# q times k-transposed for 96 heads on one core: which pieces of a block and of a head move at the same time

## The chip, the cores and the metric

The kernel runs on one NeuronCore of a Trainium2 chip. Its time is the device time in microseconds, and the median of three runs is what counts. A core has TensorE (PE) for matmuls, VectorE (DVE), ScalarE (ACT) and GpSimd (POOL) for elementwise work, SyncE (SP), which here only issues DMAs, and sixteen DMA engines that carry all traffic between DRAM and the on-chip memory SBUF.

## The reference

For 8 x 12 = 96 heads, q and k are 1024 x 64 in float32, and each head's output is the 1024 x 1024 matrix of all dot products, in float32:

```python
return np.einsum('bhid,bhjd->bhij', q, k).astype(np.float32)
```

So 50.3 MB are read and 402.7 MB are written.

## The kernel before

**Blocks.** The heads are worked through in blocks of 2, 2, 4, 8 and then five times 16 heads (`sizes`; the blocks have the numbers 0 to 8). Each engine's instructions are written out in the order in which it runs them; an engine waits for another by counting semaphores (`Engine.run`, `Engine.wait`).

**Loads.** A block's q (x = 0) and k (x = 1) are loaded by one DMA each into `x_sb` (`Block.load`, L161). The rows of a block are taken as 128 equal pieces, one for each SBUF partition; in a block of 16 heads a piece is 128 rows of 64 floats, 32 KB, so one head is eight pieces and partition p holds piece p. The first blocks are loaded by SP into a free output buffer or into `x_sb`. The loads of the blocks of 16 are issued from ScalarE's queue, q at head 1 and k at head 7 of the block before (L411; `LOADS` for the early ones), and each waits until the casts have read what it overwrites.

**Cast and transpose.** The matmul needs the 64 values of a row along partitions, so q and k are turned. GpSimd casts to float16, four instructions of 32 partitions to each chunk, into one of three `half` buffers (`cast_quads`, L210). VectorE then transposes every 32 x 32 square of a chunk in one instruction (`transpose_quads`, L229) and writes with a stride into `qT` or `kT`. A block of 16 takes four of these for q and four for k, done while the block before is computed (`TURNS`, L408), and the first head of a block waits for all of them. The first two blocks are transposed by TensorE instead (L243).

A partition's quad (32 partitions) decides where its rows go: heads 0 to 7 of a block land on rows 0 to 63 of `qT` and `kT`, heads 8 to 15 on rows 64 to 127.

**Scores.** For each head (`scores`), TensorE loads 128 rows of q as weights (L308) and multiplies them with k in two pieces of 512 (L311); with eight weight loads this gives the 1024 x 1024 result. The weights are every eighth row of the head, so that output partition m gets rows 8m to 8m+7. The PSUM halves take two of the eight parts each, and ScalarE copies each 128 x 2048 half to the output buffer (L288), four copies to a head. There are three output buffers `o_sb` of 4 MB.

**Stores.** When a head is copied, SP issues one DMA of 4096 KB (L301). Output partition p holds the contiguous 32 KB of rows 8p to 8p+7, so again partition p is piece p of the head:

```python
dma = nc.sync.dma_start(
    out=of[self.first + n].rearrange("(p t) j -> p (t j)", p=P),
    in_=buf.rearrange("p t j -> p (t j)"),
)
```

ScalarE's first copy into a buffer waits until the store that last used it has landed.

Of the kernel before, what the change touches and what calls it, by code (L numbers as in the profile page):

```python
# [8 lines left out]
P = 128  # L9
# [50 lines left out]
def kernel(  # L60
# [6 lines left out]
    nc = tc.nc  # L67

    B, H, S, D = q.shape
    NT = S // P  # L70
# [4 lines left out]
    of = out.rearrange("b h i j -> (b h) i j")  # L75
# [3 lines left out]
    NMAX = max(sizes)  # L79
# [26 lines left out]
    class Ring:  # L106


        def __init__(self, bufs):
            self.bufs, self.n = bufs, 0  # L110
            self.busy = [[] for _ in bufs]
# [11 lines left out]
    n, at = S * D // P * 2, 8 * S // 2  # L123
# [13 lines left out]
    class Block:  # L137
        def __init__(self, i, first, N):
            self.i, self.first, self.N = i, first, N
            self.by_pe = i < PE_BLOCKS  # L140
            self.R = N * S // P
            self.elems = self.R * D
            self.cut = max(1, -(-self.R * 32 // CHUNK))
            self.raw = [None] * 2
            self.landed = [[] for _ in range(2)]
            self.rows = [None] * 2
            self.halves = {}
            self.qk = qk_sb[i % 2]
            self.ready = []
            self.over = []  # L150

        def load(self, x, eng, landing=None):
            events = []
            if self.raw[x] is None:
                at = x * self.elems if self.i == EARLY else 0
                self.raw[x] = x_sb[:, at : at + self.elems]
                landing = input_landing[x]
                events = list(input_busy)
            src = flat[x][self.first * S : (self.first + self.N) * S]
            eng.wait(events)  # L160
            dma = eng.eng.dma_start(  # L161
                out=self.raw[x], in_=src.rearrange("(p r) d -> p (r d)", p=P)
            )
            self.landed[x].append(landing.start(dma))

        def load_head(self, n, x, eng, landing):
# [54 lines left out]
        def transpose_quads(self, x, part, c):  # L221
            buf, cast, busy = self.halves.pop((x, part, c))
            n, m = self.N * S // 4, self.R // self.cut
            dst = self.qk[x][:, part * n : (part + 1) * n].rearrange(
                "c (i r) -> c r i", i=32
            )[:, c * m : (c + 1) * m]
            before = blocks[self.i - 2].over if self.i >= 2 else []
            done = dve.run(
                lambda: nc.vector.transpose(  # L229
                    out=dst, in_=buf.rearrange("p (r i) -> p r i", i=32)  # L230
                ),
                [cast] + before,
            )
            busy.append(done)
            self.ready.append(done)
# [17 lines left out]
            self.ready.append(done)  # L253

        def scores(self, n, side, regions, w):
            half, g = divmod(n, self.N // 2)
            cs = slice(half * D, (half + 1) * D)
            qT = self.qk[0].rearrange("c (g m t) -> c g t m", t=NT, m=P)
            kT = self.qk[1].rearrange("c (g j) -> c g j", j=S)
            buf, out_free, out_busy = outs.next()  # L260
            written = {}
            for u in range(NT // w):
                ps, ps_free, ps_busy = regions.next()
                first = True
                for tt in range(w):
                    stationary = qT[cs, g, w * u + tt]
                    done = pe.run(
                        lambda: load_weights(stationary, half * D),
                        self.ready if n == 0 and u == 0 else [],
                        signal=False,  # L270
                    )
                    for j in range(2):
                        at = tt * S + j * 512
                        done = pe.run(
                            lambda: multiply(
                                ps[:, at : at + 512],
                                stationary,
                                kT[cs, g, j * 512 : (j + 1) * 512],
                                half * D,
                            ),  # L280
                            ps_free,
                            signal=tt == w - 1 and j == 1,
                        )
                dst = buf[:, w * u : w * u + w].rearrange("p t j -> p (t j)")
                by_dve = w == 1 and u % 2
                copier = dve if by_dve else act
                copied = copier.run(
                    lambda: (nc.vector.tensor_copy if by_dve else nc.scalar.copy)(  # L288
                        out=dst, in_=ps[:, : w * S]
                    ),  # L290
                    out_free + [done],
                )
                written[copier] = copied
                ps_busy.append(copied)
                for do in side.get(u, []):
                    do()
            self.over = [done]
            sp.wait(written.values())
            if self.first + n == 0:
                sp.wait(blocks[EARLY].landed[0])  # L300
            dma = nc.sync.dma_start(  # L301
                out=of[self.first + n].rearrange("(p t) j -> p (t j)", p=P),
                in_=buf.rearrange("p t j -> p (t j)"),
            )
            out_busy.append(store_landing[id(buf)].start(dma))

    def load_weights(stationary, at):
        return nc.tensor.ldweights(stationary, tile_position=(at, 0))  # L308

    def multiply(dst, stationary, moving, at):  # L310
        return nc.tensor.add_instruction(  # L311
            mybir.InstMatmult(
                name=nc.get_next_instruction_name(),
                ins=[nc.tensor.lower_ap(moving), nc.tensor.lower_ap(stationary)],
                outs=[nc.tensor.lower_ap(dst)],
                start_tensor_calc=True,
                stop_tensor_calc=True,
                ldweights=False,
                tile_position=(at, 0),
                tile_size=(D, P),  # L320
            )
        )
# [33 lines left out]
    for x in range(2):  # L356
# [7 lines left out]
                out=ident,  # L364
                in_=ident,
# [100 lines left out]
```

## Time and profile before

| | |
|---|---|
| median of 3 runs | 1062.69 us (1061.64 to 1063.31) |
| the profiled execution: its time, its span | 1062.84 us, 1061.0 us |
| DMA | 453.21 MB, mean 427 GB/s |
| ScalarE copies (L288), 128 x 2048 | 380, mean 1868 ns |
| VectorE transposes (L229), 128 x 2048 | 22 to qT, mean 9478 ns; 22 to kT, mean 9539 ns |
| GpSimd casts (L210), 32 x 2048 | 176, mean 1888 ns |
| store of a head, 4096 KB, issue to landing | 96, median 21.8 us |
| load of a block of 16, 4096 KB | 5 of q and 5 of k, median 24.1 and 24.3 us |

The page divides the span into 40 slices: each digit of an engine's row is its busy share of a slice in tenths, and the row of GB/s is what the DMA engines moved. The chain of waits follows the work back from the last instruction to what released each step. In a row of the waits stand the engine and line that waited, what it waited for, the microseconds in all, how often, and the longest. A row of the table by stretches has the stretch, its length, each engine's busy time and instructions, the granted TensorE clock, the DMA share and the GB/s. A queue's name with q (ACTq, SPq) is an engine's own sequencer, which issues the DMAs.

### The profile page before, as it was taken

To read this page: it belongs to the slowest core of one execution; us is meant where nothing else is said; L and a number is where in the kernel's file an instruction comes from. 1 tells how busy PE (TensorE), PEld (TensorE's weight loads), DVE (VectorE), ACT (ScalarE), POOL (GpSimd) and SP (SyncE) were. 2 spreads that over 40 slices of the span, in tenths; PEclk is the share of its full clock that TensorE was granted. 3 is DMA by queue.
4 is the path that set the end of the run, shared out by engine and by line. 5 is a ranking of instruction groups with operands and counts; after the bars stand their busy time and mean duration, and the time that the engine had idled before them with its cause. 6 is when DMAs were issued, how large, how long until landed. Compare 5 with 4: busy or idle time off the path is not lost.

```text
span 1061.0 us, 3307 instructions
## 1 busy us (share of the span) xinstructions
PE 700.2 (66%) x1568; PEld 127.3 (12%) x800; DVE 431.0 (41%) x55; ACT 697.1 (66%) x386; POOL 354.2 (33%) x206
## 2 busy tenths in 40 slices
PE   6876744957477748567765856775584777778770
PEld 1111100111011101011111101111110111111110
DVE  2995939029193009339003907600761920000000
ACT  4766655857477747567756756775675777777771
POOL 7927465056380028064006509100913700000000
DMA  9999999999999999999999999999999999999997
GB/s 376 434 435 435 434 434 434 416 421 432 431 434 434 435 429 428 426 435 432 432 422 434 435 427 433 433 434 423 433 429 432 435 434 431 434 434 431 432 431 322
DMA packets 17009, 453.21 MB, mean 427 GB/s; under 512 B 1888, under 2 KB 1888, under 8 KB 2912
## 3 DMA queue, kind: packets, MB, share of 16 engines
q1 hardware_dynamic: 14976, 410.00, 89.7%
q10 hardware_dynamic: 2016, 42.99, 9.8%
q8 instruction: 9, 0.15, 0.0%
q14 instruction: 8, 0.07, 0.0%
HBM read 50.33 MB, written 402.65 MB: 427 GB/s over the span
## 4 chain that ended last, share of the span: by engine, by line
DMA 65%; ACT 16%; PE 7%; DVE 5%; POOL 4%; issue 1%; ACTq 0%; SPq 0%
DMA out_dram<-o_sb 60%; ACT o_sb L288 16%; PE ps_all L311 7%; DVE kT L229 4%; POOL half L210 3%; DMA x_sb<-in_k_dram 2%; DMA x_sb<-in_q_dram 2%; DVE qT L229 1%; DMA o_sb<-in_q_dram 0%; PE ps_all L243 0%; POOL qT L181 0%; DVE kT L250 0%; ACT kT L250 0%; ACTq L36 0%; SPq L169 0%
## 5 line engine op out<-in xcount | busy, mean ns | idle before, releaser
L288 ACT COPY o_sb<-ps_all 128x2048 f32<-128x2048 f32 (+1 forms) x384 | 694.8, 1859 | 333.5 <-DMA out_dram<-o_sb 290.2
L311 PE MATMUL ps_all<-kT,qT 64*128 64x512 f16 x1536 | 696.1, 617 | 328.6 <-ACT o_sb L288 312.8
L210 POOL CAST half<-x_sb 32x2048 f16<-32x2048 f32 x176 | 332.3, 1888 | 482.1 <-DMA x_sb<-in_q_dram 302.2
L229 DVE STREAM_TRANSPOSE qT<-half 128x2048 f16<-128x2048 f16 x22 | 202.6, 9478 | 268.1 <-POOL half L210 268.1
L229 DVE STREAM_TRANSPOSE kT<-half 128x2048 f16<-128x2048 f16 x22 | 202.5, 9539 | 137.5 <-POOL half L210 137.5
L308 PEld LDWEIGHTS <-qT 64*128 64x128 f16 x768 | 124.2, 162 | 897.4 <-issue 878.0
L229 DVE STREAM_TRANSPOSE kT<-kT 128x1024 f16<-128x1024 f16 x2 | 9.4, 4870 | 0.0
L229 DVE STREAM_TRANSPOSE qT<-qT 128x1024 f16<-128x1024 f16 x2 | 9.2, 4780 | 0.0
L210 POOL CAST qT<-o_sb 32x1024 f16<-32x1024 f32 x8 | 8.3, 1035 | 1.2 <-DMA o_sb<-in_q_dram 0.8
L210 POOL CAST kT<-o_sb 32x1024 f16<-32x1024 f32 x8 | 8.3, 1035 | 0.5
L250 DVE COPY qT<-ps_all 128x1024 f16<-128x1024 f16 x2 | 2.4, 1224 | 11.1 <-PE ps_all L243 11.1
L288 DVE COPY o_sb<-ps_all 128x1024 f32<-128x1024 f32 x4 | 4.9, 1225 | 4.4 <-PE ps_all L311 4.4
L243 PE MATMUL ps_all<-ident,qT 128*128 128x128 f16 x16 | 2.1, 311 | 6.8 <-POOL qT L181 6.7
L250 ACT COPY kT<-ps_all 128x1024 f16<-128x1024 f16 x1 | 1.0, 1012 | 4.8 <-PE ps_all L243 4.8
L181 POOL CAST qT<-o_sb 128x512 f16<-128x512 f32 x4 | 2.3, 615 | 3.7 <-DMA o_sb<-in_q_dram 3.7
L250 ACT ACT_TABLE_LOAD x1 | 1.3, 1283 | 2.8 <-issue 2.8
L250 DVE COPY kT<-ps_all 128x1024 f16<-128x1024 f16 x1 | 1.2, 1225 | 4.4 <-PE ps_all L243 4.4
L243 PE MATMUL ps_all<-ident,kT 128*128 128x128 f16 x16 | 2.0, 305 | 0.7 <-ACT o_sb L288 0.7
L181 POOL CAST kT<-o_sb 128x512 f16<-128x512 f32 x4 | 2.4, 618 | 0.3 <-DMA o_sb<-in_q_dram 0.3
L243 PEld LDWEIGHTS ps_all<-ident,qT 128*128 128x128 f16 x16 | 1.5, 141 | 7.1 <-POOL qT L181 7.1
L243 PEld LDWEIGHTS ps_all<-ident,kT 128*128 128x128 f16 x16 | 1.5, 136 | 3.3 <-POOL qT L210 1.6
L359 POOL MEMSET ident<- 128x128 f16 x1 | 0.2, 205 | 0.5 <-SPq L98 0.5
(5 smaller groups left out, 0.7 us busy)
## 6 DMA issues: line engine op xcount, KB each, us to landing
out_dram<-o_sb SPq DMA_DIRECT2D x96, 4096.0 KB, 21.8
x_sb<-in_q_dram ACTq DMA_DIRECT2D x5, 4096.0 KB, 24.1
x_sb<-in_k_dram ACTq DMA_DIRECT2D x5, 4096.0 KB, 24.3
x_sb<-in_q_dram SPq DMA_DIRECT2D x1, 2048.0 KB, 14.6
x_sb<-in_k_dram SPq DMA_DIRECT2D x1, 2048.0 KB, 19.5
o_sb<-in_k_dram ACTq DMA_DIRECT2D x4, 256.0 KB, 4.8
o_sb<-in_q_dram SPq DMA_DIRECT2D x4, 256.0 KB, 5.1
o_sb<-in_q_dram SPq DMA_DIRECT2D x1, 1024.0 KB, 8.2
```

Of the source, the lines that this page charges most:

```text
L181: lambda: nc.gpsimd.tensor_copy(out=rows[:, :, h], in_=self.raw[x][:, h * n : (h + 1) * n].rearrange("p (r d) -> p r d", d=D),),
L210: lambda: nc.gpsimd.tensor_copy(out=dst[q0 : q0 + 32].rearrange("p (r d) -> p r d", d=32), in_=raw[32 * b : 32 * b + 32, c * m : (c + 1) * ...
L229: lambda: nc.vector.transpose(out=dst, in_=buf.rearrange("p (r i) -> p r i", i=32)),
L243: lambda: nc.tensor.transpose(t_ps[:, t], rows[:, t], ident),
L250: lambda: copy(out=dst, in_=t_ps.rearrange("c t m -> c m t")), [done]
L288: lambda: (nc.vector.tensor_copy if by_dve else nc.scalar.copy)(out=dst, in_=ps[:, : w * S]),
L308: return nc.tensor.ldweights(stationary, tile_position=(at, 0))
L311: return nc.tensor.add_instruction(mybir.InstMatmult(name=nc.get_next_instruction_name(), ins=[nc.tensor.lower_ap(moving), nc.tensor.lower ...
L359: cleared = gps.run(lambda: nc.gpsimd.memset(ident, 0.0))
```

## The change

For blocks of 16 heads (`spread`), the piece that goes with a partition is another one. Partition p = 8e + b, with e from 0 to 15 and b from 0 to 7, now holds piece 16b + e of the block (loads) or of the head (stores), where it held piece 8e + b. If a DMA engine e carries the partitions 8e to 8e+7 in order, the sixteen engines now move sixteen neighbouring pieces at a time, and before moved pieces that lie eight apart. The DRAM side of these DMAs has the shape 16 x 8 x 32 KB instead of 128 x 32 KB; the SBUF side stays 128 x 32 KB. The smaller blocks keep the old order for both loads and stores.

All else follows from it. In a load the partitions of e hold parts of all even heads (e below 8) or of all odd heads, so heads now alternate between rows 0 to 63 and rows 64 to 127 of `qT` and `kT` (`scores`). The transposes write to other places, so that k's columns stand in order and the weights (every eighth column of `qT`) give output partition 8e + b the rows of piece 16b + e. No instruction is added or removed, and every engine has its instructions in the order that it had.

```diff
+            self.spread = N == NMAX
...
-            dma = eng.eng.dma_start(
-                out=self.raw[x], in_=src.rearrange("(p r) d -> p (r d)", p=P)
-            )
+            if self.spread:
+                src = src.rearrange("(b e r) d -> e b (r d)", b=NT, e=P // NT)
+            else:
+                src = src.rearrange("(p r) d -> p (r d)", p=P)
+            dma = eng.eng.dma_start(out=self.raw[x], in_=src)
...
-            dst = self.qk[x][:, part * n : (part + 1) * n].rearrange(
-                "c (i r) -> c r i", i=32
-            )[:, c * m : (c + 1) * m]
+            if self.spread:
+                src = buf.rearrange("p (r e b) -> p r e b", e=4, b=NT)
+                if x == 0:
+                    dst = self.qk[x].rearrange("c (b f q e t) -> c q f t e b", b=NT, q=2, e=4, t=NT)
+                    dst = dst[:, part, c * m // NT : (c + 1) * m // NT]
+                    src = src.rearrange("p (f t) e b -> p f t e b", t=NT)
+                else:
+                    dst = self.qk[x].rearrange("c (b q e r) -> c q r e b", b=NT, q=2, e=4)
+                    dst = dst[:, part, c * m : (c + 1) * m]
+            else:
+                dst = self.qk[x][:, part * n : (part + 1) * n]
+                dst = dst.rearrange("c (i r) -> c r i", i=32)[:, c * m : (c + 1) * m]
+                src = buf.rearrange("p (r i) -> p r i", i=32)
...
-                lambda: nc.vector.transpose(
-                    out=dst, in_=buf.rearrange("p (r i) -> p r i", i=32)
-                ),
+                lambda: nc.vector.transpose(out=dst, in_=src),
...
-            half, g = divmod(n, self.N // 2)
+            if self.spread:
+                g, half = divmod(n, 2)
+            else:
+                half, g = divmod(n, self.N // 2)
...
-            dma = nc.sync.dma_start(
-                out=of[self.first + n].rearrange("(p t) j -> p (t j)", p=P),
-                in_=buf.rearrange("p t j -> p (t j)"),
-            )
+            dst, src = of[self.first + n], buf.rearrange("p t j -> p (t j)")
+            if self.spread:
+                dst = dst.rearrange("(b e t) j -> e b (t j)", b=P // 16, t=NT)
+            else:
+                dst = dst.rearrange("(p t) j -> p (t j)", p=P)
+            dma = nc.sync.dma_start(out=dst, in_=src)
```

## The prediction

> **What bounds the kernel now.** I read the page first: busy shares, the forty slices, then the chain.
>
> ```profile
> span 1061.0 us, 3307 instructions
> ...
> DVE 2995939029193009339003907600761920000000
> ...
> DMA  9999999999999999999999999999999999999997
> GB/s 376 434 435 435 434 434 434 416 421 432 431 434 434 435 429 428 426 435 432 432 422 434 435 427 433 433 434 423 433 429 432 435 434 431 434 434 431 432 431 322
> ...
> DMA 65%; ACT 16%; PE 7%; DVE 5%; POOL 4%; issue 1%; ACTq 0%; SPq 0%
> ```
>
> No compute engine is busy for more than 66% of the span, while the DMA row is full in all slices but the last. The chain is mostly stores. The page's 453.21 MB at 433 GB/s, the rate of the quiet stretch 880 to 1030, would take 1046.7 us; so 1061.0 - 1046.7 = 14.3 us go to start, end and dips.
>
> Next the waits, for the cover that the compute has:
>
> ```profile
> ACT o_sb L288 <- DMA out_dram<-o_sb: 290.2, 85, 12.0
> ...
> DVE qT L229 <- POOL half L210: 268.1, 5, 70.8
> ...
> DVE kT L229 <- POOL half L210: 137.5, 5, 32.7
> ```
>
> ScalarE waits 290 us for a free output buffer: it makes a head in four copies of 1.87 us (7.5 us), a store takes about 9.7 us. A faster engine gains nothing; a slower one costs only where the cover ends. That place stands in the chain in order of time:
>
> ```profile
> 118.08 23.96 DMA x_sb<-in_k_dram
> ...
> 149.85 36.75 DVE kT L229 x4
> ...
> 186.65 1.94 PE ps_all L311 x4
> ```
>
> The first block of sixteen starts when its four kT transposes end. Its first store (store 16, counted from 0) is issued at 196.08; store 15 lands at 197.58 on the first DMA engine and at 199.72 on the last. In the records of single packets the fastest engine takes up store 16 without a gap, 1.1 us after that issue, so it has next to nothing to spare here, and the slowest engine 2.1 us.
>
> Then the stretches:
>
> ```profile
> 200.00:220.00 20.00, 12.66 (x29) 2.26 (x14) 0.00 (x0) 12.23 (x7) 0.00 (x0) 1.00 1.00 405
> ...
> 370.00:390.00 20.00, 11.04 (x26) 1.94 (x12) 0.00 (x0) 10.90 (x6) 0.00 (x0) 1.00 0.99 421
> ...
> 880.00:1030.00 150.00, 112.30 (x249) 20.12 (x124) 0.00 (x0) 111.13 (x62) 0.00 (x0) 1.00 1.00 433
> ...
> 1054.00:1061.00 7.00, 0.00 (x0) 0.00 (x0) 0.00 (x0) 0.00 (x0) 0.00 (x0) 1.00 0.08 33
> ```
>
> The dips are at loads. In the packet records, which these rows sum up, most 32 KB store packets take exactly 1,213 ns and all 12,288 average 1,214.8; the 1,280 load packets average 1,253.6, stretched late in a load. 16 x 32,768 bytes in 1,213 ns are 432 GB/s: each engine is at its own floor, with 3 or 4 ns of overlap between packets. And one engine is slow: in the landing records it falls 0.06 to 0.08 us further behind per store from 250 us on, and ends at 1059.75 while the others end between 1053.8 and 1056.9. It sets the end.
>
> **The change part by part.** Sums are against the profiled execution: 1062.84 us, which is 1061.0 of span and 1.8 around it, 0.15 above the median of 1062.69.
>
> *Addresses.* Bytes, transfers and 32 KB packets stay; what changes is which pieces move at once: sixteen neighbours (32 KB apart) instead of sixteen at 256 KB. It holds for 80 stores and for the ten 4096 KB loads. Gain at most: all stretch above 1,213 ns goes, 768 x 1.8 ns + 80 x 40.6 ns = 4.6 us per engine, and the slow engine falls in with the next one, about 3 us. Loss at most: the nearest row is four store packets at 202.2 us which took 2,406 to 2,419 ns, twice the floor, together; were all so, the 369 MB moved after 196 us (80 stores and 8 loads of 4.19 MB, 855 us at 432 GB/s) would take 855 us more. I take 0, the value nearest to the steady rows: with pieces 256 KB apart almost every store packet is at the floor, so addresses cost it nothing now, and the slow lane keeps its pace in stretches with and without loads.
>
> *Dealing to engines.* The DRAM side of these transfers becomes 16 x 8 x 32 KB while the SBUF side stays 128 rows. The trace does not name an engine's partitions, so whether each engine keeps its rows is open. I take that it does, at 0; else it is rival two.
>
> *The transposes.* 40 of the 48 (L229, blocks of sixteen) write with other steps: kT 64 x 4 x 8 with steps of 2, 256 and 2,048 bytes, qT 8 x 8 x 4 x 8 with 128, 2, 16 and 2,048. Today the innermost step is 64, 128 or 256 bytes by block size: 4,695 to 4,879 ns for 1,024 columns, 9,514 to 9,561 and 9,311 to 9,689 for 2,048, so 4.55 to 4.76 ns per element throughout. A fourfold step moved nothing, so I take 0 for 2,048 bytes too. Bounds: below, a VectorE copy into contiguous qT (L250), 1,224 ns for 1,024, so 2.45 us; above, an estimate of twice today's 9.19 us pitch. Faster gains nothing (DMA is full). Slower by d costs 4d at 186.65 less about 2 us of queue. At later block starts kT ends at 327.6; its first head's copies can't begin before a buffer is free at 356.4, so TensorE needs it near 354, and 12 us of stores are queued beyond: 38 us are covered. Longer qT hardly moves the k load: issued at 258.97, it waits on ScalarE's queue, copies behind it, for the last q cast (L210), now over at 255.2; but kT (from 290.85) must wait for a qT that runs on. Twice as long, the first start has qT until 168.4 and kT until 242, 55 - 2 = 53 us late, and each of four later ones has kT until 379 instead of 366, 13 us: 1062.7 + 53 + 52 = 1168.
>
> *Halves and issue.* Heads alternate between the two 64-row halves; matmul and weight loads keep count and steps. Nothing, covered by about 2 us per head in which the copies wait for stores; without it, 768 loads of 162 ns would show in part. Issue: another dimension may lift 332 ns to at most the 443 of another form, 96 x 0.1 us on SP and 10 on ScalarE. Stores are issued 12 us ahead of need and ScalarE idles 290 us: 0; uncovered, 11 us. The end is the last store after 1038.2: unchanged.
>
> Sum: 1062.84 + 0 = 1062.8, at the median 1062.7.
>
> **The rivals.**
>
> *One: faster.* Neighbouring pieces spread better over the memory, the late stretch of loads goes and the slow engine catches up. For it: load packets stretch in nearly all later loads, and dips to 405 and 421. Against: stores at the floor. Half of 4.6 and half of 3: 1062.7 - 3.8 = 1058.9; at most 1055.1. [...]
>
> *Two: slower, engines meet.* If the outer 16 makes each engine take eight consecutive partitions, and two engines then draw on one path into SBUF, their packets stretch. For it: the two sides have unlike outer sizes for the first time, and doubled packets exist. Against: their cause is not shown. As no engine ever idles, it decides from a mean packet 3 ns over 1,214.8; a tenth longer gives 1062.7 + 85 = 1148, double 1918. [...]
>
> *Three: slower, transposes.* 2,048-byte steps are dearer. From d = 1 us it shows: 1062.7 + 2 = 1065; at half again as long, d = 4.6, 16 us: 1079; double: 1168. Against: three steps at one price.
>
> **How the numbers follow.** 0.2% (2.1 us) is about what a measurement can tell from no change. No effect: 0.31 (1060.6 to 1064.8). Rival one: 0.28. Two: 0.23. Three, or addresses a little worse: 0.18. Faster 0.28, same 0.31, slower 0.41. Predicted 1062.7. Range: below to 1055, where rival one ends; above to 1110, which holds rival three but for its doubled end and the mild end of rival two, and leaves out some 0.18.
>
> **What would show it.** The L229 groups near 9.5 us; the quiet stretch at 433 GB/s and the median store's 21.8 us to landing; 405 and 421 at loads gone if rival one holds; PE waiting for kT longer than 10.3 us if three. Rival two: DMA full at well under 433 GB/s from 200 us on, landings above 30 us. I am wrong if the dealing or the memory, neither of which the trace of before shows, does matter.

## The result

The changed kernel takes 1371.86 us (median of four times, 1365.99 to 1380.12); the kernel before, on the same chip, 1062.62 (four times, 1061.64 to 1063.31). The ratio is 1.292, with a 95% interval of 1.284 to 1.300: 309 us slower. The profiled execution of the changed kernel has a time of 1365.99 us and a span of 1364.2, so 303.2 of span are to be found.

The profile page of the changed kernel, its DMA rows, its shares by queue, its chain and three groups, in the page's own columns:

```profile
span 1364.2 us, 3307 instructions
...
DMA  9999999999999999999999999999999999999996
GB/s 385 439 355 415 374 435 268 302 298 334 349 331 260 300 341 320 328 377 270 273 315 363 355 343 357 287 321 337 311 275 342 356 345 375 319 336 316 346 313 224
...
q1 hardware_dynamic: 14976, 410.00, 87.1%
q10 hardware_dynamic: 2016, 42.99, 11.0%
...
DMA 72%; ACT 12%; PE 6%; DVE 4%; POOL 3%; issue 1%; SPq 0%; ACTq 0%
...
L302 ACT COPY o_sb<-ps_all 128x2048 f32<-128x2048 f32 (+1 forms) x384 | 694.9, 1859 | 626.9 <-DMA out_dram<-o_sb 580.8
...
L242 DVE STREAM_TRANSPOSE qT<-half 128x2048 f16<-128x2048 f16 x22 | 200.6, 9389 | 395.5 <-POOL half L213 395.5
L242 DVE STREAM_TRANSPOSE kT<-half 128x2048 f16<-128x2048 f16 x22 | 202.0, 9463 | 249.4 <-POOL half L213 249.4
...
out_dram<-o_sb SPq DMA_DIRECT2D x96, 4096.0 KB, 32.9
x_sb<-in_q_dram ACTq DMA_DIRECT2D x5, 4096.0 KB, 34.8
x_sb<-in_k_dram ACTq DMA_DIRECT2D x5, 4096.0 KB, 34.3
```

From the page of the kernel before, its shares by queue and its copies:

```profile
q1 hardware_dynamic: 14976, 410.00, 89.7%
q10 hardware_dynamic: 2016, 42.99, 9.8%
...
L288 ACT COPY o_sb<-ps_all 128x2048 f32<-128x2048 f32 (+1 forms) x384 | 694.8, 1859 | 333.5 <-DMA out_dram<-o_sb 290.2
```

The engines of the DMA row are as full as before and carry the same 453.21 MB, but at 260 to 377 GB/s from the seventh slice up to the last. The third and fifth slices, at about 68 to 102 and 136 to 171 us, already drop to 355 and 374: there the first two loads of sixteen heads run, beside stores that still have the old shape. ScalarE copies at its old 1859 ns and waits 580.8 us for stores, twice the 290.2 of before. VectorE's longer waits for the casts (395.5 and 249.4 us against 268.1 and 137.5) lead back to loads as well: the casts wait 429.2 us for q loads where they waited 302.2. So the transfers themselves are longer.

The records of single packets say by how much. A 32 KB packet of a store took 1214.8 ns in the mean before and takes 1521.3 now; a packet of a 4096 KB load 1253.6 and 1839.6. Each of the sixteen engines moves 768 such store packets and 80 such load packets: 768 x 306.5 ns + 80 x 586 ns = 235 + 47 = 282 us. The rest is idle engines: the shares of queues 1 and 10 add up to 98.1% of 1364.2 us against 99.5% of 1061.0, so 26 us idle against 5, 21 us more. 282 + 21 = 303, the whole difference.

The stretched packets are not alike. Of the store packets after 215 us (10,222, mean 1578 ns), nearly half still take 1,211 to 1,230, and one in ten takes 2,540 or more: as if an engine were at its floor, or near half speed, or changed over within a packet.

### The profile page after: what moved, and what is told of

Its sections match the earlier page's. It is cut to its first block, busy times and chain, and to the rows that moved or that the text cites. A ratio compares the mean times of both kernels' runs of the same rounds, so it can differ in the third digit from the quotient of the medians.

```text
span 1364.2 us, 3307 instructions
## 1 busy us (share of the span) xinstructions
PE 700.5 (51%) x1568; PEld 125.7 (9%) x800; DVE 428.6 (31%) x55; ACT 697.2 (51%) x386; POOL 354.4 (26%) x206
## 2 busy tenths in 40 slices
DMA packets 17009, 453.21 MB, mean 332 GB/s; under 512 B 1888, under 2 KB 1888, under 8 KB 2912
## 4 chain that ended last, share of the span: by engine, by line
DMA 72%; ACT 12%; PE 6%; DVE 4%; POOL 3%; issue 1%; SPq 0%; ACTq 0%
DMA out_dram<-o_sb 67%; ACT o_sb L302 12%; PE ps_all L327 5%; DVE kT L242 3%; POOL half L213 3%; DMA x_sb<-in_q_dram 2%; DMA x_sb<-in_k_dram 2%; DVE qT L242 1%; DMA o_sb<-in_q_dram 0%; PE ps_all L254 0%; POOL qT L184 0%; DVE kT L261 0%; ACT kT L261 0%; ACTq L36 0%; SPq L172 0%
## 5 line engine op out<-in xcount | busy, mean ns | idle before, releaser
L302 ACT COPY o_sb<-ps_all 128x2048 f32<-128x2048 f32 (+1 forms) x384 | 694.9, 1859 | 626.9 <-DMA out_dram<-o_sb 580.8
L213 POOL CAST half<-x_sb 32x2048 f16<-32x2048 f32 x176 | 332.5, 1889 | 718.8 <-DMA x_sb<-in_q_dram 429.2
L242 DVE STREAM_TRANSPOSE qT<-half 128x2048 f16<-128x2048 f16 x22 | 200.6, 9389 | 395.5 <-POOL half L213 395.5
L242 DVE STREAM_TRANSPOSE kT<-half 128x2048 f16<-128x2048 f16 x22 | 202.0, 9463 | 249.4 <-POOL half L213 249.4
```

What stands on the lines that cost most here:

```text
L213: lambda: nc.gpsimd.tensor_copy(out=dst[q0 : q0 + 32].rearrange("p (r d) -> p r d", d=32), in_=raw[32 * b : 32 * b + 32, c * m : (c + 1) * ...
L242: lambda: nc.vector.transpose(out=dst, in_=src),
```

## The experiments

**Shape or addresses.** The change does two things to a transfer: other pieces meet each other in DRAM, and the DRAM side has the outer sizes 16 x 8 in place of 128. The first experiment keeps every address of the kernel before, and its transposes, and writes only the DRAM side as 16 x 8 pieces. The second writes both sides as 128 x 1 x 32 KB, by the same way of issuing. The third keeps 128 in its stores and brings the addresses that move at once close together; for that an output partition holds other rows of a head, and its 32 KB go out as eight pieces of 4 KB.

In the excerpts `dst` and `src` stand for the two sides as in the kernel before, and `dma_as` issues the same DMA with each side's dimensions written out as [step, count], in elements. Only the lines that differ are shown, without their conditions: they hold for the blocks of sixteen.

```diff
 first (dims of the DRAM side; loads alike, the other way round)
-dma = nc.sync.dma_start(out=dst, in_=src)
+dma = dma_as(nc, nc.sync, dst, src, [[65536, 16], [8192, 8], [1, 8192]], [[8192, 128], [1, 1], [1, 8192]])
 second
+dma = dma_as(nc, nc.sync, dst, src, [[8192, 128], [1, 1], [1, 8192]], [[8192, 128], [1, 1], [1, 8192]])
 third
-qT = self.qk[0].rearrange("c (g m t) -> c g t m", t=NT, m=P)
+qT = self.qk[0].rearrange("c (g t m) -> c g t m", t=NT, m=P)
-dma = nc.sync.dma_start(out=of[...].rearrange("(p t) j -> p (t j)", p=P), in_=buf.rearrange("p t j -> p (t j)"))
+dma = nc.sync.dma_start(out=of[...].rearrange("(t p) j -> p t j", p=P), in_=buf)
```

What was expected of the first:

> The kernel before with every piece at its old place (partition 8e+b holds piece 8e+b), and only the DRAM side of the 80 stores and ten loads of the blocks of sixteen written as 16 x 8 x 32 KB instead of 128 x 32 KB. Three theories. Dealing (an outer 16 gives each DMA engine eight consecutive partitions, and engines then meet on the way in and out of SBUF): as slow as the changed kernel, 1330 to 1420 us, and about 330 to 340 GB/s from the first store of a block of sixteen on. Addresses (sixteen neighbouring pieces at a time are slow in DRAM): 1060 to 1066 us, 433 GB/s in the quiet stretch, because the addresses are the old ones. Form (a DMA whose sides are not both the plain 128 rows is carried out in a slower way): slow as well, 1330 us or more; the next run separates it from dealing.

of the second:

> The same as the run with the outer 16, with old addresses, but both sides of those DMAs are 128 x 1 x 32 KB: three dimensions as in the changed kernel, outer size 128 as before. Dealing: 1061 to 1065 us, no different from before, since both outer sizes are 128. Addresses: the same, 1061 to 1065 us. Form (three dimensions, or anything but the plain two-dimensional DMA, is slow): 1330 us or more.

and of the third:

> The outer size stays 128 on both sides, but what moves at a time in a store are neighbours: output partition p holds rows p, 128+p, ... of a head (4 KB each), so that engines with eight partitions each are 32 KB apart, as in the changed kernel, and all work inside 512 KB of a head. Loads are as before. The weights are read as 128 consecutive columns of qT. Addresses: slow, 1300 us or more. Dealing: no such loss; only the cost of eight times as many packets, which the 2 KB and 8 KB packets at the start of the trace of before (84 and 309 to 314 ns) put at about 160 ns for 4 KB or 5% of a store: 1062 to 1110 us. Form: between, since the DMA has three dimensions with equal outer sizes; 1300 us or more if any third dimension is slow.

Measured: the first 1348.1 us (1323.88 and 1372.32), the second 1063.6 (ten times, 1062.59 to 1065.79; ratio 1.0012, interval 1.0002 to 1.0021), the third 1106.07 (once). The rate by slices, the first kernel (its profiled time is the 1372.32), then the second, then the third:

```profile
GB/s 398 428 335 417 386 433 279 313 327 337 283 281 318 310 338 325 339 343 305 353 334 335 312 354 297 327 309 354 326 285 322 335 343 271 317 345 359 305 335 216
```

```profile
GB/s 383 432 420 434 434 434 433 404 429 434 434 431 434 431 416 433 432 434 434 433 431 432 432 418 433 433 434 419 430 428 432 432 434 433 434 433 429 434 434 307
```

```profile
GB/s 380 436 435 430 431 431 436 400 422 412 412 406 406 403 412 412 397 422 409 404 399 422 408 404 419 406 405 402 421 409 405 416 403 406 406 405 403 407 404 372
```

With the addresses of before, outer size 16 alone gives a row like that of the changed kernel; what the new addresses add, if anything, is lost in the 48 us between the first kernel's two times. A third dimension with outer size 128 gives the row of before, and a loss of about 0.1%. The third kernel falls to about 405, and its packets say why: they are eight of 4 KB where there was one of 32 KB, and take 163.7 ns each, so 1,310 for 32 KB against 1,215. That is the price of small packets; 95 in 100 take 168 ns or less, so next to none is doubled, although what moves at once lies within one half megabyte if the engines keep step. So the cost belongs to the shape 16 x 8 and not to the way of issuing, and no cost of the addresses shows.

**Is it that two engines share a path?** If the sixteen engines are dealt the sixteen outer pieces, an engine has eight consecutive partitions, and by the predicted rival two of them draw on one path. This can be put to the test without the shape: to a DMA of exactly sixteen partitions the records show sixteen 32 KB packets and sixteen 4-byte ones, one of each for an engine if they are dealt evenly. The first of three such kernels issues each store as eight DMAs of partitions i, i + 8, ..., i + 120 and the old addresses. The other two read fixed sets of sixteen partitions: every eighth (0 to 120) or every seventh (0 to 105), so that their outputs repeat sixteen partitions and are not the result.

```diff
+for i in range(8):
+    dma = nc.sync.dma_start(out=dst[i::8], in_=src[i::8])       # first
+    dma = nc.sync.dma_start(out=dst[i::8], in_=src[0:121:8])    # second
+    dma = nc.sync.dma_start(out=dst[i::8], in_=src[0:106:7])    # third
```

> Each store of a block of sixteen is cut into eight DMAs of sixteen partitions each, b, 8+b, 16+b and so on, at their old addresses; each engine then carries one 32 KB piece of each. [...] If only some of the engines meet it stays under 1500. Addresses: 1060 to 1080 us, as the pieces that move together are the old ones, 256 KB apart. Form: two-dimensional with equal outer sizes, so 1060 to 1080 us.

> A measurement of the path by itself; what is stored is not the result. Every store of a block of sixteen is eight DMAs of sixteen partitions, and all eight read the same sixteen, 0, 8, 16 to 120, so that the output of these heads repeats one eighth of the partitions; compute and bytes moved are as before. [...] Store packets of 2,426 ns throughout, a store in 19.4 us, 216 GB/s with a full DMA share, and 1062 + 80 x 9.7 = 1838 us. If what slowed the earlier run was the small DMAs, or a store's number of them, rather than the path: 1565 us again, and the same in the run with the step of 7.

> The same, with the sixteen partitions 0, 7, 14 to 105 for all eight DMAs; what is stored is not the result. [...] So twelve engines at 1,213 ns and four at 2,426, a quarter of the store packets doubled and almost none in between; the slow four set the store's time, so again near 1838 us, but with a DMA share of (12 x 0.5 + 4) / 16 = 0.63 between loads, where the step of 8 has 1.0. [...]

Measured: 1565.58, 1880.72 and 1794.84 us. The stretches of the second of them, between loads (length, busy time of each engine, granted clock, DMA share, GB/s):

```profile
700.00:800.00 100.00, 33.29 (x75) 5.96 (x37) 18.34 (x3) 33.15 (x20) 4.90 (x3) 1.00 1.00 203
1500.00:1600.00 100.00, 34.39 (x76) 6.01 (x38) 0.00 (x0) 33.30 (x19) 0.00 (x0) 1.00 1.00 204
```

and of the third:

```profile
700.00:800.00 100.00, 36.30 (x80) 6.48 (x40) 0.00 (x0) 36.35 (x20) 0.00 (x0) 1.00 0.63 215
1500.00:1600.00 100.00, 36.31 (x80) 6.46 (x40) 0.00 (x0) 36.34 (x20) 0.00 (x0) 1.00 0.63 216
```

In the second every store packet of these stretches is doubled: they take 2,548 to 2,575 ns, most of them 2,551 to 2,573, the engines are never idle, and 203 GB/s is 12.7 for each engine, 25.4 for two together. The third decides. In these stretches 74% of its store packets take 1,213 to 1,229 ns and a quarter 2,395 to 2,418: by that count twelve engines of the one kind and four of the other. If the twelve wait for the four, the DMA share is (12 x 1,221 + 4 x 2,405) / (16 x 2,405) = 0.63, and 0.63 was measured. As the two kernels differ only in which partitions the stores read, what doubles a packet is on that side. Which partitions share a path the two runs do not single out: the twelve and four of the expectation, and with them its 0.63, rest on a grouping that the author assumed and no run shows. Both times came within 3% of the 1838 us that was expected.

The author had expected the first near 1840 us too, as if two engines met in every packet. It came to 1565.58: its store packets after 215 us average 1,964 ns, not 2,560. So not every packet was doubled; how its engines come out of step, no run shows.

**Do the engines of the changed kernel meet in this way?** No record names an engine. But an engine's packets follow each other so closely (each starts from 14 ns before to 40 ns after the end of the last) that most can be strung together by their times, and a 4-byte packet ends each store. In the changed kernel this gives, after 215 us, 976 strings of the eight packets that one engine moves for one store. In 756 of them some of the eight, but not all, take over 1,300 ns. The commonest kinds, with the long packets as x:

```
.... ....   197 strings
...x ...x   117
x... x...    75
xx.. xx..    74
..xx ..xx    60
xxx. xxx.    51
.xxx .xxx    30
```

In 407 of the 756 the second four are as the first four; in random order 8% would be. Without the strings in which two packets could have come next it is 177 of 348. In the kernel before, 1,214 of 1,223 strings have no long packet, and in the padded one 1,187 of 1,210; none there has two like halves with a long packet. That speaks for eight packets that go by two paths, four and four; and the kinds come in mirror pairs, as if one engine of a pair were a little ahead of the other. Which partitions the packets belong to, the records do not say.

**One part alone.** Outer size 16 on the eighty stores alone, and on the ten loads alone (old addresses, as in the first kernel above):

```diff
 stores alone
+dma = dma_as(nc, nc.sync, dst, src, [[65536, 16], [8192, 8], [1, 8192]], [[8192, 128], [1, 1], [1, 8192]])
 loads alone
+dma = dma_as(nc, eng.eng, self.raw[x], src, [[8192, 128], [1, 1], [1, 8192]], [[65536, 16], [8192, 8], [1, 8192]])
```

> Old addresses, and the outer 16 on the 80 stores alone; the ten loads keep the plain 128 rows. Dealing: stores are where most packets stretch. In the changed kernel the 10,222 store packets after 215 us average 1,578 ns against 1,214, which is 639 packets per engine x 364 ns = 233 us; so 1290 to 1310 us if the stores stretch as much without the turned loads, and loads of the plain form take their 1,213 to 1,260 ns again where no store is beside them.

> Old addresses, and the outer 16 on the ten 4096 KB loads alone. Dealing: load packets near 1,840 ns as in the changed kernel instead of 1,254, which is 80 packets per engine x 586 ns = 47 us; with some loss at the casts that wait for a load, 1100 to 1130 us. Stores of the plain form stay at 1,213 ns except beside a load.

Measured: stores alone 1126.97 us, a miss; loads alone 1129.99, as expected. The kernel before took 1064.17 beside them. The loads' packets averaged 1,918 ns instead of 1,254, and the stores' 1,230: 80 x 664 ns + 768 x 15 ns = 65 us of the 66 measured. The stores alone, by slices:

```profile
GB/s 388 430 427 430 431 437 433 276 299 282 331 385 352 367 391 393 416 405 417 431 433 414 425 422 417 425 431 418 421 432 411 431 430 430 431 429 416 429 432 313
```

They begin as slowly as in the changed kernel (276 to 299) and are back above 410 before the middle. The landing records hint how. These are the sixteen engines' landings of one store, in us after the first of them:

```
kernel before,   store 60: 0 .01 .04 .15 .54 .57 .90 .93 | 1.25 1.28 1.34 1.38 1.87 2.21 2.28  4.00
changed kernel,  store 60: 0 .67 .78 2.29 2.64 2.71 3.02 | 3.72 3.83 4.26 4.67 4.78 10.05 13.41 13.97  16.50
stores alone,    store 20: 0 3.63 6.58 8.74 8.82 9.18 9.27 | 10.05 11.17 11.22 11.84 12.48 12.79 15.05 15.33  17.27
stores alone,    store 75: 0 .28 .31 .56 .67 .82 1.07 | 4.80 5.07 5.11 5.14 5.20 5.61 5.67 5.86  9.90
stores alone,    store 85: 0 .09 .13 .52 .58 1.53 2.24 | 4.88 5.30 5.30 5.34 5.38 5.45 5.55 5.95  10.95
```

Once it runs at full rate, the landings stand in two groups, 4.8 to 4.9 us apart. Four packets at 1.213 us are 4.85. So about half of the engines seem to be half a store ahead of the others. If, as the strings above suggest, an engine's first four packets go by one path and its last four by another, partners that are half a store apart do not meet; no run tests it.

**Why the parts did not add up.** 63 + 66 is 129, not the roughly 300 of both together (the expectation below has 64, counted from 1062.62). Three runs were to tell why: the stores alone again, with the first block's two loads turned as well, and with the other eight loads turned as well.

```diff
 stores, and the loads of the first block of sixteen
-            if self.N == NMAX:
+            if self.N == NMAX and self.first == 16:
 stores, and the loads of the other blocks
-            if self.N == NMAX:
+            if self.N == NMAX and self.first > 16:
```

> The kernel with outer size 16 on its stores alone, once more, unchanged (1126.97 us in its one time; the rate began at 276 to 299 GB/s after store 16 and was back above 410 by the middle). What is open: outer size 16 on the stores alone costs 64 us and on the ten loads alone 66, both together about 300, though the packets are the same. Three ways to account for it. Back: in a kernel of turned stores the engines drift out of step until the two of a path no longer meet, and each turned load, which overtakes the stores on the same engines, puts them in step again. Start: only what the first turned loads leave behind counts, and lasts. Chance: whether the engines come out of step differs from execution to execution. Back and Start: 1120 to 1135 again, with the same recovery. Chance: somewhere else between 1100 and 1350, and unequal among its own times.

> Outer size 16 on the stores and on the two loads of the first block of sixteen heads alone (they run at about 60 to 150 us, before the first turned store at 196). By parts alone it would be 1127 + 66 x 2/10 = 1140 us. Back: 1130 to 1160, with the rate above 410 GB/s from the middle on, since no turned load comes later. Start: near the whole change, 1300 to 1372, with no recovery.

> Outer size 16 on the stores and on the eight loads of the other four blocks, the first block's two loads as before. By parts alone: 1127 + 66 x 8/10 = 1180 us. Back: near the whole change, 1290 to 1372, the rate falling again or staying low at each pair of loads. Start: about 1180, with the recovery of the stores alone.

Measured: the same kernel as at 1126.97 now took 1214.05 and 1310.48 us; with the first loads 1161.28 and 1279.33; with the later loads 1299.08 and 1332.09. Back and Start asked for 1120 to 1135 again, and Back for at most 1160 with only the first loads turned; so neither alone accounts for the gap, and Chance stands. Its spread was then measured by itself:

> The kernel with outer size 16 on its stores alone a third time, for how far its times lie apart (so far 1126.97, 1214.05 and 1310.48 us). Chance: the engines of a path come out of step in some executions, early or late, and not in others, so its times lie unevenly between 1100 and 1330, over 50 us from the lowest to the highest, while the kernel before stays within 3 us. If one price per store held, all would lie within 10 us of one another.

Six times: 1111.19, 1139.53, 1223.00, 1228.09, 1238.11 and 1324.94, a spread of 214 us at a granted clock of 1.00 in each, while the kernel before stayed within 1061.81 to 1063.91 in eleven. The profiled one of these (1238.11) goes well and then loses it again, by slices and then by stretches:

```profile
GB/s 390 427 438 430 434 432 345 311 282 345 383 402 425 404 429 415 404 345 350 350 397 265 284 350 327 346 355 399 332 357 400 378 344 275 310 351 366 364 409 316
```

```profile
420.00:460.00 40.00, 22.20 (x50) 3.96 (x25) 17.75 (x2) 24.16 (x14) 24.80 (x14) 1.00 1.00 424
460.00:500.00 40.00, 25.19 (x57) 4.46 (x28) 19.03 (x3) 25.23 (x15) 5.38 (x3) 1.00 1.00 418
500.00:540.00 40.00, 25.20 (x56) 4.54 (x28) 29.00 (x4) 23.55 (x14) 30.19 (x16) 1.00 1.00 375
540.00:580.00 40.00, 21.78 (x48) 3.89 (x24) 7.76 (x1) 21.59 (x12) 0.00 (x0) 1.00 0.99 356
```

All nine times of the stores alone lie between 1111 and 1325 us, with a median of 1223. So the +63 was one draw from a range of about +48 to +262. Taking that whole range and the loads' +66, the changed kernel's +309 lies inside it (+114 to +328), towards its upper end. What stays open is why the changed kernel is steadily there (1366 to 1380 in four times). The kernels with more turned loads lie higher and closer together, which would fit turned loads that keep putting partners in step; with two times for each of them, and a good stretch that ended after 510 us, when a load with the old shape had landed at about 503, that is not shown. No version here beats the kernel before.

## Why the prediction was wrong, point by point

**What bounds the kernel** was right, and the point from which rival two was to decide ("as no engine ever idles, it decides from a mean packet 3 ns over 1,214.8") as well: 282 of the 303 us are packet time.

**Addresses, at 0,** held as far as the runs can tell: the old addresses are about as slow with outer size 16 (1323.88 and 1372.32), and with close addresses but outer size 128 hardly a packet is doubled. The bound of 855 us above that term came from four packets at 2,406 to 2,419 ns. Those are the size of the doubled packets of the every-seventh kernel (2,395 to 2,418). But they stand in the kernel before, where the store packets average 1,214.8 ns, just after a load began (its first packets are at 201.8 us); what doubled them stays open.

**Transposes, at 0,** held: 9,389 and 9,463 ns against 9,478 and 9,539, so a step of 2,048 bytes costs nothing, and rival three falls.

**Halves and issue, at nothing,** held as far as the groups show: weight loads 160 ns (162 before), matmuls 617 as before, ScalarE's copies 1,859 as before. The bound on the issue was too low: a store takes 538 ns to issue in the median against 332, and a load of a block of sixteen 543 to 609 against 334 to 371, where 443 was to be the most. That stays covered: the padded kernel's stores take 472 ns to issue, and it lost about 1 us in all.

**Dealing to engines is the step that failed:** "I take that it does, at 0", of each engine keeping its rows. The term was not 0 but 260 to 309 us (1323.88 and 1372.32 with outer size 16 alone against 1063.6 with 128): with outer size 16 on one side packets stretch as if two engines met on a path. That each engine then has a run of consecutive partitions is the author's account, and no trace names an engine's partitions. What the runs show is that the shape alone is enough (1348.1 against 1063.6), that the partitions which a store reads decide how many packets double (all in the every-eighth kernel, a quarter in the every-seventh), that the long packets stand in like halves of four (407 of 756 strings), and that the landings come in two groups half a store apart (4.8 to 4.9 us). The prediction had this as rival two, with a path shared by two engines as its assumption, and with the signs that came true (under 433 GB/s from 200 us on, landings above 30 us), and with its two ends: a tenth longer 1148, double 1918. The stores' packets came out 25% longer and the loads' 47%, between those ends. Two errors of judgement made the miss. The 0 was given no reason: the steady rows, which carried the 0 for the addresses, hold no DMA of that size with unequal outer sizes, so they could not speak on it. And the range stopped at 1110, above which rival two had nearly all its prices.

**Rival one, faster,** falls with the addresses: the kernel is slower, and the shortest packets of a store are still at 1,211 to 1,213 ns.

## What to carry to other kernels

Give both sides of a large DMA the same outer size, 128 partitions, even where one side then needs a dimension of 1: here the order of pieces in DRAM showed no cost of its own (1371.86 us with the new order, 1323.88 and 1372.32 with the old), while an outer size of 16, with the new order, cost 29%. Before a change of shape in a kernel whose DMA engines are always busy, ask whether each engine will keep its partitions, and give the case in which engines meet its real price. Where a part alone costs far less than its share, time it several times before a reason is sought: here one kernel ran from 1111 to 1325 us.

## What the runs showed that was not expected

- A doubled 32 KB packet takes 2.0 to 2.1 times as long: 2,395 to 2,418 ns where a quarter of the packets are doubled, 2,551 to 2,573 where all are, against 1,213. Two packets in 2,405 ns are 27.2 GB/s, as is one in 1,213 (27.0), so if the doubled packets come from pairs of engines, one engine by itself already gets what such a pair gets together.
- With outer size 16 on the stores alone the engines can, by the landings, fall into a rhythm half a store apart, at 410 to 433 GB/s; and a stretch at 418 to 424 GB/s can end again, at 375 and then 356. The same program then has times up to 214 us apart.
- A 32 KB piece cut into eight 4 KB packets costs 8% more engine time (1,310 against 1,215 ns), of which 43 us, 4%, came through in the whole kernel.
